# Four loads of q by GpSimd around DMA engine 4, where two had been

## The chip, the cores and the metric

The kernel runs on one core of one Trainium2 chip. The metric is the device time of one execution in microseconds (us), lower is better. The profiled span is about 1.8 us shorter than the time of the same run.

## The reference

Rotary embedding of q and k, then for each batch and head all products of queries with keys. There is no softmax.

```python
batch, seq, heads, dim = 16, 512, 16, 64            # all float32
q_rot = concatenate([q1*cos - q2*sin, q1*sin + q2*cos])   # q1, q2: halves of dim; k likewise
scores = einsum('bshd,bthd->bsht', q_rot, k_rot)    # 16 x 512 x 16 x 512
```

Input is 67 MB, output 268 MB. So this is first of all a kernel that writes.

## The kernel before

A step makes the scores of 128 queries of one batch (four steps to a batch, 64 in all), collects them in one of three stages of 4 MB, and stores that with one DMA issued by SyncE. A stage is used again only when its store has landed whole. A batch of q or k is loaded as one DMA of 128 rows of 16 KB, one row per partition, one batch ahead.

```python
    for i in range(C, NST):                     # the steps from batch 1 on
        ...
        if i % C == C - 2:
            load("q", i // C + 2)
        elif i % C == C - 1:
            load("k", i // C + 3)
    # in scores(i, p), after the last heads of a step:
            dma(SP, nc.sync, o_v[b, i % C], st, f"out{s}", reads=[("st", s, x) for x in range(HP)])
```

One of the 16 DMA engines is slow, and the kernel already takes some work off it: in two batches GpSimd loads 120 rows on fifteen engines, and SyncE the last 8.

```python
    RELIEVED = {("q", 6): 0, ("q", 12): 1}
    SLOW = 4

    def load(which, b):
        ...
        if (which, b) not in RELIEVED:
            dma(SP, nc.sync, ..., dram[which][b], sem, writes=rows + rest)
            return
        n, E, F = 120, C * H * D, C * H * D // 2
        x = RELIEVED[which, b]
        plan.add(POOL, None, (), rows)           # waits, then resets GpSimd's cursor over the engines
        # a dummy of SLOW + 1 = 5 rows: the cursor then stands on engine 5
        ...
        dma(POOL, nc.gpsimd, dst, src, "cursor", writes=[("scratch", x)])
        # 120 rows in halves of 8 KB, on the 15 engines from there: all but engine 4
        ...
        dma(POOL, nc.gpsimd, dst, src, f"part{x}", writes=rows)
        # the last 8 rows, on engines 0 to 7
        dma(SP, nc.sync, t[n:]..., d[n:], sem, writes=rest)
```

## Time and profile before

| what | value |
|---|---|
| time, median of 3 runs | 802.25 us (802.22 to 802.61) |
| profiled span | 799.2 us, of one run of 801.0 us (1.2 us under the median) |
| DMA busy | nine tenths or more in every slice but the first and the last |
| PE, ACT, DVE busy | 86%, 70%, 68% of the span |
| ACT waiting for a store to free a stage | 102.6 us |

The views that carry the argument are in the prediction and are read there. Two things of how to read them. The share of one DMA engine is seen twice in a trace: each DMA leaves sixteen landing records, one for each engine's part, and every packet has a start and a length. Packets don't say which engine moved them. But each starts 3 or 4 ns before the end of the one before it on the same engine, and so they can be strung into sixteen **lanes**. An undisturbed packet of 32 KB (a row of a store) takes 1213 ns, of 16 KB (a row of a load) 611, of 8 KB 309.

### The profile page before, as it was taken

The page shows a single profiled execution, that of the slowest core. Times are in us where ns is not written, and L with a number is a line of the kernel's source. Part 1 is how long each engine was busy: PE and PEld are TensorE (multiplying, and loading weights), DVE is VectorE, ACT ScalarE, POOL GpSimd, SP SyncE. Part 2 cuts the span into 40 slices and gives each one's busy share as a digit, 9 for nine tenths or more (in the row PEclk, how much of TensorE's full clock was granted, in tenths as well). Part 3 has the DMA queues.
Part 4 walks back from the last instruction along what each step waited for, and adds up shares of the span by engine and source line. Part 5 has one row for each costly group of instructions (what it writes and reads, how often), then busy time and mean ns, then how long its engine had stood idle before and what let it go on. Part 6 is the DMA issues. An engine that isn't in the chain of part 4 may idle for free.

```text
span 799.2 us, 8189 instructions
## 1 busy us (share of the span) xinstructions
PE 686.3 (86%) x3072; PEld 297.0 (37%) x3072; DVE 545.2 (68%) x516; ACT 562.5 (70%) x647; POOL 3.5 (0%) x10
## 2 busy tenths in 40 slices
PE   3989998897979979798797987979979799899960
PEld 2444443343434434343343433424434343334320
DVE  6999988586856858577585775857858477585300
ACT  3978886785857858587585875757857687678760
POOL 0000000000000000000000000000000000000000
PEclk9999999898998989899898998988989899899995
DMA  8999999999999999999999999999999999999994
GB/s 346 421 422 424 428 432 427 427 436 430 431 428 431 411 431 426 439 430 433 432 426 433 431 427 431 431 425 420 430 426 436 433 429 434 431 434 403 441 423 180
DMA packets 18033, 335.87 MB, mean 420 GB/s; under 512 B 1904, under 2 KB 3184, under 8 KB 4208
## 3 DMA queue, kind: packets, MB, share of 16 engines
q1 hardware_dynamic: 17120, 331.62, 97.3%
q0 software_dynamic: 608, 3.93, 1.2%
q10 hardware_dynamic: 288, 0.13, 0.1%
q8 instruction: 6, 0.10, 0.0%
q14 instruction: 11, 0.09, 0.0%
HBM read 67.24 MB, written 268.44 MB: 420 GB/s over the span
## 4 chain that ended last, share of the span: by engine, by line
DMA 47%; PE 36%; DVE 8%; ACT 6%; issue 1%; ACTq 0%; DVEq 0%; SPq 0%
DMA out_dram<-st 47%; PE ps L393 27%; PE bank L344 9%; ACT st L402 6%; DVE st L319 3%; DVE part L319 2%; DVE k_sb L319 2%; DVE q_sb L319 1%; DMA sin_t<-in_sin_dram 0%; DVE kT L362 0%; DVE qT L362 0%; ACTq L237 0%; ACT ss_t L439 0%; ACT ss_t L438 0%; ACTq L110 0%
## 5 line engine op out<-in xcount | busy, mean ns | idle before, releaser
L402 ACT COPY st<-ps 128x1024 f32<-128x1024 f32 x512 | 495.7, 1018 | 198.6 <-DMA out_dram<-st 102.6
L393 PE MATMUL ps<-kT,qT 64*128 64x512 f32 x2048 | 544.0, 648 | 71.6 <-ACT st L402 71.6
L393 PEld LDWEIGHTS ps<-kT,qT 64*128 64x128 f32 x2048 | 183.0, 196 | 261.3 <-issue 133.9
L362 DVE COPY qT<-bank 128x512 f32<-128x512 f32 x118 | 81.6, 691 | 199.4 <-PE bank L344 199.4
L344 PEld LDWEIGHTS bank<-ident,q_sb 128*128 128x128 f32 x480 | 55.3, 151 | 102.0 <-issue 98.5
L344 PE MATMUL bank<-ident,q_sb 128*128 128x128 f32 x480 | 86.5, 307 | 1.0 <-DVE q_sb L319 1.0
L344 PEld LDWEIGHTS bank<-ident,k_sb 128*128 128x128 f32 x480 | 50.5, 141 | 94.1 <-DVE k_sb L319 47.5
L344 PE MATMUL bank<-ident,k_sb 128*128 128x128 f32 x480 | 78.7, 287 | 1.6 <-DVE k_sb L319 0.8
L362 ACT COPY kT<-bank 128x512 f32<-128x512 f32 x122 | 72.4, 597 | 6.7 <-PE bank L344 6.7
L319 DVE TENSOR_TENSOR part<-q_sb,ss_t 128x1024 f32<-128x1024 f32 x60 | 73.5, 1225 | 3.1
L319 DVE TENSOR_TENSOR q_sb<-q_sb,cos_t 128x1024 f32<-128x1024 f32 x60 | 73.5, 1225 | 2.1
L319 DVE TENSOR_TENSOR k_sb<-k_sb,cos_t 128x1024 f32<-128x1024 f32 x60 | 73.5, 1225 | 2.0
L319 DVE TENSOR_TENSOR k_sb<-k_sb,part 128x1024 f32<-128x1024 f32 x60 | 73.5, 1225 | 2.1
L319 DVE TENSOR_TENSOR part<-k_sb,ss_t 128x1024 f32<-128x1024 f32 x60 | 73.0, 1216 | 0.3
L319 DVE TENSOR_TENSOR q_sb<-q_sb,part 128x1024 f32<-128x1024 f32 x60 | 72.9, 1216 | 0.0
L344 PE MATMUL bank<-ident,st 128*128 128x128 f32 x64 | 10.8, 318 | 13.3 <-DVE st L319 13.3
L344 PEld LDWEIGHTS bank<-ident,st 128*128 128x128 f32 x64 | 8.2, 161 | 18.6 <-DVE st L319 16.8
L319 DVE TENSOR_TENSOR part<-st,ss_t 128x1024 f32<-128x1024 f32 x8 | 9.8, 1222 | 6.4 <-ACT ss_t L439 6.0
L319 DVE TENSOR_TENSOR st<-st,part 128x512 f32<-128x512 f32 x16 | 11.1, 691 | 0.5
L319 DVE TENSOR_TENSOR st<-st,cos_t 128x1024 f32<-128x1024 f32 x8 | 9.8, 1225 | 0.3
L362 ACT COPY qT<-bank 128x512 f32<-128x512 f32 x10 | 5.7, 615 | 3.5 <-PE bank L344 3.5
L362 DVE COPY kT<-bank 128x512 f32<-128x512 f32 x6 | 4.1, 683 | 0.0
(11 smaller groups left out, 5.5 us busy)
## 6 DMA issues: line engine op xcount, KB each, us to landing
out_dram<-st SPq DMA_DIRECT2D x60, 4096.0 KB, 25.0
k_sb<-in_k_dram SPq DMA_DIRECT2D x15, 2048.0 KB, 27.2
q_sb<-in_q_dram SPq DMA_DIRECT2D x13, 2048.0 KB, 29.7
out_dram<-st SPq DMA_DIRECT2D x16, 1024.0 KB, 13.2
q_sb<-in_q_dram POOLq DMA_DIRECT2D x2, 1920.0 KB, 29.7
st<-in_k_dram SPq DMA_DIRECT2D x1, 1536.0 KB, 8.9
st<-in_q_dram SPq DMA_DIRECT2D x1, 1536.0 KB, 12.1
st<-in_k_dram SPq DMA_DIRECT2D x1, 512.0 KB, 4.6
```

What stands on the lines that cost most here:

```text
L319: plan.add(DVE, one(lambda: nc.vector.tensor_tensor(o, a, b, op=op)), reads, writes, also=more)
L344: done = [nc.tensor.transpose(bank[:, x, :], srcs[x], ident) for x in range(4)]
L362: plan.add(engine, one(lambda: copy(out=dst, in_=src)), [("bank", m)], keys)
L393: nc.tensor.matmul(out=ps[:, r, :], lhsT=lhs[lo:hi, :], rhs=rhs[lo:hi, :], start=True, stop=True)
L402: plan.add(ACT, one(lambda: nc.scalar.copy(out=so, in_=si)), [("ps", y)], [("st", s, p)])
```

## The change

The intent: engine 4 ends last by 7 us. Take more rows from it, by relieving four loads rather than two, spaced evenly; and let the 8 rows that remain go to engines 8 to 15 in every second of them, so that engine 4 doesn't get one and engines 0 to 7 don't get all.

```diff
-    RELIEVED = {("q", 6): 0, ("q", 12): 1}
+    RELIEVED = {("q", 5): 0, ("q", 8): 1, ("q", 11): 2, ("q", 14): 3}
+    tiny = [0]
     SLOW = 4
 ...
+        def move_cursor(k):                      # the dummy, now of k rows
 ...
+        def halves(lo, hi, keys, sem):           # rows lo to hi by GpSimd, in halves of 8 KB
 ...
         plan.add(POOL, None, (), rows)
 ...
-        dma(POOL, nc.gpsimd, dst, src, f"part{x}", writes=rows)
-        dma(SP, nc.sync, t[n:].rearrange("p c (h d) -> p c h d", h=H), d[n:], sem, writes=rest)
+        if x % 2:
+            move_cursor(8)
+            halves(n, P, rest, f"rest{x}")       # the rest on engines 8 to 15
+        move_cursor(SLOW + 1)
+        halves(0, n, rows, f"part{x}")
+        if not x % 2:
+            dma(SP, nc.sync, t[n:].rearrange("p c (h d) -> p c h d", h=H), d[n:], sem, writes=rest)
```

More of the change, by code (lines that the diff above doesn't have):

```diff
@@ L277, in load @@
         x = RELIEVED[which, b]
-        plan.add(POOL, None, (), rows)
-        src = bass.AP(q.tensor, 512 * x, [(512, SLOW + 1), (64, 2), (1, 2)])
-        dst = scratch[: SLOW + 1, 4 * x : 4 * x + 4].rearrange("p (a b) -> p a b", a=2)
-        dma(POOL, nc.gpsimd, dst, src, "cursor", writes=[("scratch", x)])
-        d = dram[which][b]
-        src = bass.AP(d.tensor, d.offset + F, [(E, n), (-F, 2), (1, F)])
-        dst = bass.AP(t.tensor, t.offset + F, [(t.ap[0][0], n), (-F, 2), (1, F)])
-        dma(POOL, nc.gpsimd, dst, src, f"part{x}", writes=rows)
-        dma(SP, nc.sync, t[n:].rearrange("p c (h d) -> p c h d", h=H), d[n:], sem, writes=rest)
+        d = dram[which][b]
+        def move_cursor(k):
+            y = tiny[0]
+            tiny[0] += 1
+            src = bass.AP(q.tensor, 512 * y, [(512, k), (64, 2), (1, 2)])
+            dst = scratch[:k, 4 * y : 4 * y + 4].rearrange("p (a b) -> p a b", a=2)
+            dma(POOL, nc.gpsimd, dst, src, "cursor", writes=[("scratch", y)])
+        def halves(lo, hi, keys, sem):
+            src = bass.AP(d.tensor, d.offset + lo * E + F, [(E, hi - lo), (-F, 2), (1, F)])
+            v = t[lo:hi]
+            dst = bass.AP(v.tensor, v.offset + F, [(v.ap[0][0], hi - lo), (-F, 2), (1, F)])
+            dma(POOL, nc.gpsimd, dst, src, sem, writes=keys)
+        plan.add(POOL, None, (), rows)
+        if x % 2:
[5 more added lines that the diff above has]
+            dma(SP, nc.sync, t[n:].rearrange("p c (h d) -> p c h d", h=H), d[n:], sem, writes=rest)
     def src_keys(which, n):
```

## The prediction

> **What bounds the kernel now.** I read the page first (what moved the data and how evenly), then the chain of waits in the last 110 us, then the totals of waits, then the single landings and packets in the trace.
>
> The page, sections 2, 3 and 4 (mean busy share of the 16 DMA engines in 40 slices, GB/s of the same slices, queues, traffic, and the chain by engine):
>
> ```profile
> DMA  8999999999999999999999999999999999999994
> GB/s 346 421 422 424 428 432 427 427 436 430 431 428 431 411 431 426 439 430 433 432 426 433 431 427 431 431 425 420 430 426 436 433 429 434 431 434 403 441 423 180
> ...
> q1 hardware_dynamic: 17120, 331.62, 97.3%
> q0 software_dynamic: 608, 3.93, 1.2%
> ...
> HBM read 67.24 MB, written 268.44 MB: 420 GB/s over the span
> ...
> DMA 47%; PE 36%; DVE 8%; ACT 6%; issue 1%; ACTq 0%; DVEq 0%; SPq 0%
> ```
>
> The DMA engines are busy in every slice but the last; PE (86%) and ACT (70%) are not full. 335.87 MB at about 430 GB/s is 781 us of the 799.2 us span. The traffic does not change here, so only its distribution over engines can be worth anything. The last slice (180 GB/s) is where that shows: some engines have finished, others have not.
>
> The chain of waits from 690 us (start, length, what):
>
> ```profile
> 695.19 22.85 DMA out_dram<-st
> ...
> 737.24 1.13 PE ps L393 x4
> ...
> 746.35 21.44 DMA out_dram<-st
> ...
> 767.87 5.93 ACT st L402 x7
> ...
> 774.20 1.09 ACT st L402
> ```
>
> A 4 MB store takes 22.85 and 21.44 us to land. The last store is issued at 775.32 and lands 21.65 us later, at 796.97; 2.2 us of closing work make the span. A store lands when its slowest sixteenth does. The sixteen landing records of each DMA, in us after its issue, sorted:
>
> ```
> issue   what       sixteen shares
> 508.06  store      18.40 18.43 18.52 18.54 18.55 18.56 18.68 18.91 21.01 21.16 21.27 22.22 22.37 23.51 23.55 28.48
> 558.98  store      17.50 17.52 17.64 17.70 17.76 17.89 17.96 18.39 18.95 19.12 19.50 20.69 20.94 21.35 22.05 25.18
> 679.21  store      13.52 13.57 13.62 13.68 13.69 13.81 13.89 14.31 15.19 15.47 16.22 17.26 17.42 17.59 18.11 23.97
> 775.32  last store 11.74 11.76 11.80 11.81 11.81 11.82 11.86 11.87 11.88 11.93 12.59 13.14 13.45 13.99 14.69 21.65
> ```
>
> One share is far behind: 21.65 against 14.69 for the next, **6.96 us that only one engine works in**. The packets explain it. They carry no engine number, but each starts 3 or 4 ns before the end of the one before it on its engine, so they chain into lanes. From 400 to 472 us most lanes move 26.7 to 27.05 GB/s (a 32 KB packet takes 1213 ns), and one moves 26.42, with 43 of its 80 packets slow. None of them pauses. Around the relieved load at 527 us that slow lane alone carries no 8 KB packet of the GpSimd load: it is the engine the kernel already steers around, number 4 in the code.
>
> The relief that exists (the GpSimd timeline, start and length in us; the last bracket is the wait before it):
>
> ```profile
> 228.14 0.69 POOL L237 DMA_DIRECT2D scratch<-in_q_dram  x1 [226.62 <-PE bank L344]
> 228.82 0.75 POOL L237 DMA_DIRECT2D q_sb<-in_q_dram  x1
> 526.51 0.58 POOL L237 DMA_DIRECT2D scratch<-in_q_dram  x1 [296.94 <-PE bank L344]
> 527.09 0.75 POOL L237 DMA_DIRECT2D q_sb<-in_q_dram  x1
> ```
>
> Each pulls the lag in (28.48 minus 23.55 = 4.93 us at 508; 25.18 minus 22.05 = 3.13 us at 559), and it grows back: 5.86 us at 679, 6.96 us at the end.
>
> **What the Trainium skill says.** "DMA: Bandwidth & Descriptors", section "Why a DMA increments its semaphore by 16 and not by 1": a copy uses the largest k up to 16 that divides its slowest dimension; a hardware-queue copy runs on the lowest-numbered k engines, a GpSimd one with k under 16 on k consecutive engines from a round-robin cursor. So 120 rows go to 15 engines from the cursor, and a dummy of 5 rows puts the cursor on 5, so that engine 4 is left out. The trace agrees: 480 packets of 8 KB, two a row, 16 on each of 15 lanes per load, none on the slow one. Section "Where 436 GB/s comes from" puts the ceiling at 435.2 GB/s; a clean lane of 27.05 GB/s times 16 is 433, so nothing is to be won above that. Section "Latency and other measured facts" says that engines 7 and 15 are usually slower; the trace disagrees, as the slow lane is one of the five that the 5-row dummy touches (its packets there are 16 bytes, elsewhere 8). "SBUF — State Buffer", section "SBUF: two separate sides", warns that GpSimd's descriptor writing can be blocked by VectorE; here its loads take 0.75 us to issue and 29.7 us to land, as those of SyncE do (29.7), so no sign of it.
>
> **The change, part by part.** A normal q load is 128 rows of 16 KB, 8 rows per engine.
>
> *Removed from engine 4.* Before: batches 6 and 12, 7 rows off each (the 8-row rest still puts one on it): 14. After: batches 5 and 11 in the same way (7 each), batches 8 and 14 with the rest on engines 8 to 15 (8 each): 30. The difference is 16 rows of 16,384 B = 262,144 B; at the lane's 26.42 GB/s that is **9.9 us**, all on the path, since this lane never pauses. Its end goes from 796.97 to about 787.1.
>
> *Added to the others.* Engines 0 to 3 and 5 to 7 get one row from each of two rests, before and after: nothing new. Engines 8 to 15 get one row from each of two rests, before none: 2 x 626 ns (mean of the 16 KB packets) = 1.25 us.
>
> *Who ends last then.* The next two lanes end at 775.32 + 14.69 = 790.01 and 789.31. Followed through the second relief, two lanes next behind engine 4 were one of engines 5 to 7 (it gets a single row of the rest) and one of 8 to 15 (it does not). Which is which at the end I can't tell; I give 1.25 us to the earlier: 790.0 and 790.6. They have their own backlog, so an earlier issue of the last store doesn't move them.
>
> *Cost of a relieved load.* 8 KB packets average 319 ns, 638 a row against 626: 0.1 us per load. More weight: 16 KB reads slow down in a burst when the lanes are close together and enter a load at one time (272 to 274 us, up to 1934 ns instead of 611; excess 0.75 us per engine; slice 14 shows 411 GB/s), and around 545 to 553 (0.65 us). Both follow a relief. Two more reliefs, partly with such a burst: I choose +0.7 us.
>
> *Issuing.* GpSimd gets 10 more instructions, none over 1 us, on an engine idle 99%; two SyncE issues go. Off the path.
>
> Sum: 790.6 + 0.7 = 791.3 against 796.97, **minus 5.7 us**; 802.25 - 5.7 = 796.5 us.
>
> **The rivals.** (1) *The middle lanes become the bound earlier.* The mean of the last landing over all lanes is 775.32 + 13.0 = 788.3, so even a perfect split gains 8.7 us (1.1%). If bursts follow all four reliefs and hit the late lanes, 1.5 to 2 us more: 798. For it: the bursts seen. Against: they came in other places too (75 us). (2) *Compute takes the tail.* From 719 to 746 us the chain is PE and ACT, stores 10 us apart. If that run starts no earlier, little is won: 800. Against: it begins with the store of 695.19 landing at 718.04, whose other 15 shares were in by 711.86, so it moves up by up to 6 us. (3) *Loads from GpSimd jump the queue.* They interleave with waiting stores, and the store issued at 220.74 took 30.2 us rather than 26 to 28. If a stage comes free too late, all engines pause: 1 us each, 798. Against: no lane paused there before. (4) *No late lanes but engine 4:* if the lag of the others comes from accidents early in the run, they may be reshuffled and the end nears 788.5: 794.
>
> **Range and chances.** 796.5 us, 793.8 to 799.5 in 8 of 10: the low end is rival 4, the high end rivals 1 and 3 together. Over 2% faster needs 786.2, below the perfect split: 0.01. Slower by 2% would need a new stall of 16 us: 0.02. Within 2%: 0.97.
>
> **What would show it.** The last store's largest landing falls from 21.65 to 15 or 16 us, with the gap to the next under 2 us (engine 4 no longer last); last slice above 180 GB/s; 960 8 KB packets from 120-row loads plus 32 from the two small rests, none on the slow lane; ACT's wait for stores (102.6 us in all) shorter. Wrong if the gap stays at 5 us or more (a relief removes less than counted), if idle gaps appear in the lanes, or if dips like the 411 GB/s of slice 14 follow all four loads.

## The result, and the profile after

The changed kernel took **798.6 us** (median of 4 runs, 797.49 to 799.53) against 802.24 (4 runs, 801.46 to 802.61). The ratio is 0.9955, 95% interval 0.9938 to 0.9973: within 2%, so the same by that measure, but a small gain that the interval keeps clear of zero. (Ratios are the mean time of one kernel's fast runs over that of the other's fast runs of the same rounds, so not quite the ratio of the medians quoted.) It is 2.1 us above the predicted 796.5 and inside the range. A second set of 6 runs in later rounds gave 798.98 and 0.9962.

A trace is of one run: that of before of a run of 801.0 us, 1.2 us under the median, that of the changed kernel of one of 798.9, 0.3 us over it. So between the two traces the end moves by 2.1 us only, where the medians differ by 3.6.

The page of the changed kernel, the same parts as shown of before (DMA busy in tenths and GB/s in 40 slices, queues, traffic, chain):

```profile
DMA  8999999999999999999999999999999999999995
GB/s 346 420 424 433 429 418 434 426 434 423 430 413 427 435 434 428 439 421 414 426 427 437 432 435 426 419 428 432 428 431 433 432 429 411 428 432 437 430 433 238
...
q1 hardware_dynamic: 16832, 327.42, 96.5%
q0 software_dynamic: 1376, 8.13, 2.4%
...
HBM read 67.24 MB, written 268.44 MB: 421 GB/s over the span
...
DMA 47%; PE 35%; DVE 8%; ACT 6%; issue 1%; ACTq 0%; DVEq 0%; SPq 0%
```

The last slice moved 238 GB/s where it was 180: the ends of the engines lie closer together. GpSimd's queue moved 8.13 MB where it was 3.93. But there are more dips now: slices 12, 19 and 34 (413, 414, 411) follow the loads of batches 5, 8 and 14, and 419 in slice 26 that of batch 11; before there was one deep dip after a relief, slice 14 (411), and a shallow one after the other, slice 28 (420). Before's slice 37 (403) has become 437; more of that below.

The chain of waits of the changed kernel from 690 us (start, length, what):

```profile
692.42 23.51 DMA out_dram<-st
...
717.07 1.71 PE ps L409 x4
...
745.83 19.87 DMA out_dram<-st
...
765.77 5.93 ACT st L418 x7
...
772.11 1.09 ACT st L418
```

It is the same chain. Its run of PE and ACT begins when the store of 692.42 has landed, at 715.93 (it was 718.04), and the last store is issued at 773.23 (775.32): both 2.1 us earlier.

The timeline of GpSimd in the changed kernel (start and length in us, instruction):

```profile
178.43 0.70 POOL L237 DMA_DIRECT2D scratch<-in_q_dram  x1 [176.91 <-PE bank L360]
179.12 0.75 POOL L237 DMA_DIRECT2D q_sb<-in_q_dram  x1
327.14 0.59 POOL L237 DMA_DIRECT2D scratch<-in_q_dram  x1 [147.26 <-PE bank L360]
327.73 0.57 POOL L237 DMA_DIRECT2D q_sb<-in_q_dram  x1
328.29 0.57 POOL L237 DMA_DIRECT2D scratch<-in_q_dram  x1
328.86 0.76 POOL L237 DMA_DIRECT2D q_sb<-in_q_dram  x1
```

The two forms of relief, as meant: two issues with the rest by SyncE, four with the rest by GpSimd, none over 0.8 us. In the packets of the second form, eight lanes carry 18 of 8 KB, seven carry 16, and one none.

What the change was for is in the landing records of the last store (my ordering of them, us after its issue):

```
kernel   issue    sixteen shares
before   775.32   11.74 11.76 11.80 11.81 11.81 11.82 11.86 11.87 11.88 11.93 12.59 13.14 13.45 13.99 14.69 21.65
changed  773.23   13.71 14.06 14.06 14.08 14.59 14.71 14.85 15.19 15.25 16.32 16.36 16.66 17.45 17.99 18.05 21.63
```

**Engine 4 is still last**, by 3.6 us where it was 7.0. Its end moved from 796.97 to 794.86, by 2.1 us. The prediction had it move by 9.9.

Where the rest went shows in the lanes during a relieved load. While the other fifteen engines move the 120 rows, the lane left out has only stores to do, and they are slow:

```
32 KB packets of the left-out lane in time order, ns (1213 when undisturbed)
before,  load at 228 us:  1376 1501 1558 1473 1473 1498 1500 1518 1528
changed, load at 179 us:  1551 1471 1473 1569 1444 1460 1484 1464 1484 1352
changed, load at 476 us:  1512 ... 1511 1516 1535 1506 1539 1532 ... 1335
```

Over 1213 ns a packet, this **slow spell** costs the left-out lane 2.68 and 2.07 us in the two reliefs of before, 2.71, 2.37, 2.68 and 1.72 us in the four of the changed kernel. A relief takes 7 or 8 rows off it, 4.3 to 5.0 us; 1.6 to 3.2 us of that remain. (The sums take in engine 4's ordinary slowness, packets of 1220 to 1270 ns, for as long as the load lasts. With packets over 1300 ns alone I get 2.5 and 1.4 us before, 2.6, 2.2, 2.2 and 1.3 us after.) It was there in the trace of before all along, in a stretch that I had used only to find the lane without 8 KB packets.

A second account takes all sixteen engines together. Summed over all packets and divided by 16, the time of an engine splits into packets at undisturbed speed (782.0 us before, 782.1 after), what packets took beyond that, and idle time:

```
us per engine                         before   changed
packets beyond undisturbed speed        6.2      7.8
idle from 150 to 780 us                 1.0      0.1
idle from 780 us to the last landing    8.6      5.6
sum                                    15.7     13.5
last landing                          796.97   794.86
```

(Idle time before 150 us, 2.8 us in one and 2.9 in the other, is left out, and so are the 3 or 4 ns by which packets overlap. The tail is counted to the end of the last packet, 0.47 us before its landing.) The sums differ by 2.2 us and the landings by 2.1, so nothing of size is missing. The tail got 3.0 us shorter, 0.9 us of idle went (all of it in before's slice 37, after the store of 695.19 whose last share the chain waited for), and 1.6 us came back as slower packets.

### The profile page after: what moved, and what is told of

Same layout as the page of the kernel before. It is cut to its first block, busy times and chain, and to the rows that moved or that the text cites. A ratio compares the mean times of both kernels' runs of the same rounds, so it can differ in the third digit from the quotient of the medians.

```text
span 797.1 us, 8197 instructions
## 1 busy us (share of the span) xinstructions
PE 684.3 (86%) x3072; PEld 295.4 (37%) x3072; DVE 545.2 (68%) x516; ACT 562.4 (71%) x647; POOL 8.4 (1%) x18
## 3 DMA queue, kind: packets, MB, share of 16 engines
q0 software_dynamic: 1376, 8.13, 2.4%
## 4 chain that ended last, share of the span: by engine, by line
DMA 47%; PE 35%; DVE 8%; ACT 6%; issue 1%; ACTq 0%; DVEq 0%; SPq 0%
DMA out_dram<-st 47%; PE ps L409 27%; PE bank L360 9%; ACT st L418 6%; DVE st L335 3%; DVE part L335 2%; DVE k_sb L335 2%; DVE q_sb L335 1%; DMA st<-in_k_dram 1%; DVE kT L378 0%; DVE qT L378 0%; ACTq L110 0%; DVEq L110 0%; SPq L542 0%; SPq L513 0%
## 5 line engine op out<-in xcount | busy, mean ns | idle before, releaser
L237 POOL DMA_DIRECT2D scratch<-in_q_dram x6 | 3.6, 600 | 615.4 <-PE bank L360 615.4
## 6 DMA issues: line engine op xcount, KB each, us to landing
q_sb<-in_q_dram POOLq DMA_DIRECT2D x4, 1920.0 KB, 32.6
st<-in_q_dram SPq DMA_DIRECT2D x1, 1536.0 KB, 12.2
```

Source lines behind the costliest of these rows:

```text
L237: plan.add(engine, one(lambda: e.dma_start(dst, src)), reads, writes, sem=sem, also=also)
```

## The experiments

Three questions: why does a relief give less than its rows, what do the bursts of slow loads come from, and is there a better split? My theory after the result: a lane that is left out stores slowly as long as the others load, and this eats half of what its fewer rows save. The rivals: engine 4 itself is weak there; the bursts that follow GpSimd's loads eat the gain; the place of the reliefs or the split of the rest decides.

All versions of the kernel are correct; the three bare tests (`m1`, `m2`, `m3`) store a constant, back to back, and only run loads beside it. Their outputs are wrong, which doesn't matter for the times. "End" is the last landing of the profiled run, "lead" how much later it is than the second-last lane. The profiled run is not always near the median: that of e_none took 810.07 us, the slowest of its four, and that of e_five 800.34, 1.4 us over its median.

| run | time, median (range) | ratio to before [95%] | end | lead |
|---|---|---|---|---|
| before (first rounds) | 802.24 (801.46–802.61) | | 796.97 | 6.95 |
| changed | 798.6 (797.49–799.53) | 0.9955 [0.9938, 0.9973] | 794.86 | 3.59 |
| e_after (changed, again) | 798.98 (797.85–800.78) | 0.9962 [0.9949, 0.9975] | 795.23 | 4.37 |
| e_pool16 | 805.97 (805.35–806.46) | 1.0043 [1.0026, 1.0060] | 801.84 | 6.37 |
| e_none | 806.05 (803.96–810.07) | 1.0042 [1.0026, 1.0059] | 806.15 | 4.42 |
| e_even | 799.52 (799.16–801.29) | 0.9969 [0.9950, 0.9987] | 795.38 | 3.71 |
| e_late | 797.56 (796.06–802.61) | 0.9949 [0.9906, 0.9991] | 794.45 | 2.05 |
| e_late_again | 797.12 (795.87–801.51) | 0.9945 [0.9924, 0.9965] | 794.27 | 2.69 |
| e_five | 798.98 (796.81–800.38) | 0.9955 [0.9939, 0.9971] | 796.27 | 3.38 |
| e_seven | 802.66 (801.67–806.14) | 1.0013 [0.9994, 1.0031] | 797.10 | 1.33 |
| e_store2 | 829.02 (827.68–830.37) | 1.0332 [1.0315, 1.0349] | | |

### m1_skip_each: is it engine 4?

Sixty-eight stores of 4 MB, and beside them sixteen loads of 120 rows by GpSimd that leave out engine 0, then 1, and so on.

```python
TESTS = [(e, [(0, 120, (e + 1) % 16)]) for e in range(16)]   # engine left out; first row, rows, dummy's rows
```

> Wrong results on purpose: 68 stores of 4 MB run back to back with no compute, and sixteen GpSimd loads of 120 rows leave out engine 0, 1, ... 15 in turn, one every four stores. In the changed kernel the left-out engine 4 stored slowly beside each such load: 5 to 10 packets of 32 KB at about 1490 ns instead of 1213, 1.3 to 2.6 us in all. Theory 1 (the rows still go into the partitions from which the left-out engine's stores read, only by other engines): whichever engine is left out, the lane without 8 KB packets shows such a spell, 2 to 3 us in each of the sixteen tests. Rival (it is engine 4's own weakness beside GpSimd loads): a spell in the test that leaves out engine 4 alone, under 0.5 us in the others. Also: if one lane is about 2% slower in stores alone, engine 4's weakness does not need loads or compute.

Measured: every left-out lane has the spell. Its cost was, for engines 0 to 15 in order,

```
4.46 3.79 3.75 3.94 3.64 4.70 3.73 3.02 3.50 3.43 3.40 3.87 3.13 3.10 3.98 3.74 us
```

with most stores at 1450 to 1550 ns. (How the packets are strung matters: a second program gave 3.5 to 5.0 us, single lanes up to 1.1 us apart from these, and 4.4 for engine 4.) Engine 4 is not worse than all the rest. The rival falls: any engine that is left out pays, and here, where nothing but stores fills its time, it pays 3.0 to 4.7 us of the 5.0 that 8 rows are worth.

The expectation also asked whether a lane is slow in stores alone. None is: from 727 to 748 us of this test, with only stores in flight, the sixteen lanes average 1213 to 1218 ns. In the kernel one lane is slow with only stores in flight, too (e_pool16, 280 to 300 us: 1240 ns, the other fifteen 1213). And it stops with the compute: in the trace of before, engine 4's packets take 1226 to 1268 ns until the last matmul ends at 773.7 us, and 1213 to 1218 from 775 us on. So engine 4 is not weak at storing as such; it is slow beside something else that the kernel does. What that is, no run shows.

### m2_rows: which rows, or how many?

The same with engine 4 left out and other sets of rows.

```python
TESTS = [(4, [(0, 120, 5)]), (4, [(0, 60, 5)]), (4, [(64, 60, 5)]), (4, [(0, 30, 5)]), ...,
         (4, [(8, 120, 5)]), (4, [(16, 15, 5)]), (4, [(16, 8, 8)]), ...]   # first row, rows, dummy's rows
```

> Wrong results on purpose: the same stream of stores, engine 4 left out of every GpSimd load, but the loads write different rows: 120 from 0, 60 from 0, 60 from 64, 30 from 0, 30, 60 and 90, 120 from 4 and from 8, then short ones (15 rows from 16; 8 rows from 16, 48, 0, 64 on engines 8 to 15; 4 rows from 16 and 64). Theory 1 (a port of a fixed group of partitions is shared): the extra time of the left-out lane's stores is there for the loads that cover that group and is zero for the others, so 60 from 0 and 60 from 64 differ by 2 us or more, or both have half where the group is split. Rival (any GpSimd load slows the lane that takes no part): the extra time follows the number of rows, 2.4 us for 120, 1.2 for 60, 0.6 for 30, wherever they lie.

Measured: 120 rows cost 3.90, 3.88 and 4.05 us (from row 0, 4, 8), 60 rows 2.15 and 1.86 (from 0, 64), 30 rows 0.83 to 0.95 wherever they lie, 15 rows 0.60. Which rows it is makes no difference. Eight rows on eight engines, eight left out, hardly slow a store (1230 to 1290 ns). That last point was not what the run was for, and gave the next one.

### m3_packets: packet size, queue, number of engines

```python
# rows, packets of a row, issuing engine; GpSimd starts at engine 5
TESTS = [(120, 2, "POOL"), (120, 1, "POOL"), (120, 4, "POOL"), (120, 8, "POOL"), (104, 2, "POOL"),
         (88, 2, "POOL"), (40, 2, "POOL"), (35, 2, "POOL"), (24, 2, "POOL"),
         (120, 2, "ACT"), (120, 1, "ACT"), (104, 2, "ACT"), (40, 2, "ACT"), (120, 2, "POOL")]
```

> Wrong results on purpose: the stream of stores again; beside it loads that leave engines out, by GpSimd in 120 rows cut into 2, 1, 4 and 8 packets a row, then 104, 88, 40, 35 and 24 rows (13, 11, 10, 7 and 12 engines), then by ScalarE's hardware queue in 120 rows of 2 and of 1 packets, 104 and 40 rows. Theory 2 (held in step: a left-out engine gets one empty packet for each packet of the others and then stores no faster than they do): its 32 KB stores take as long as one store plus one load packet of the others, about 1510 ns with 8 KB packets, 1820 with 16 KB, 1360 with 4 KB, 1285 with 2 KB; without empty packets, on the hardware queue, 1213. Rival (they contend for something with a fixed price): about 1500 ns whatever the packet, and also on the hardware queue; and the more engines are left out, the less each loses.

Measured, with packets of 8 KB, by the number of engines that load (the largest divisor of the rows up to 16, as the lanes confirm; the rule is in the Trainium skill, "DMA: Bandwidth & Descriptors", section "Why a DMA increments its semaphore by 16 and not by 1"):

```
engines that load            15     13     12     11     10      7
rows                        120    104     24     88     40     35
store on left-out lanes, ns 1541   1449   1434   1422   1360   1236   (mean)
```

It is the **number of engines** that load at one time that sets how slow the stores of those left out become (or the number left out, which these tests can't tell from it); the rows set how long it lasts. A repeat of 120 rows gave 1454, so the single figures are good to some 100 ns, the fall from 15 engines to 7 is not in doubt. Size: 16 KB packets 1630 where my idea of lanes held in step wanted 1820, so that idea fails; 4 KB packets 1362. From ScalarE's hardware queue, 120 rows slow the left-out lane too (1439 to 1535 in the spell), so it is nothing of GpSimd's. (The test meant with packets of 2 KB came out as 4 KB.) What the engines share there, no run shows.

### e_pool16: the same loads by GpSimd, without the relief

```diff
-        if x % 2: ...                            # all from here to the rest by SyncE
+        halves(0, P, rows + rest, f"part{x}")    # 128 rows, all 16 engines
```

> The changed kernel with the same four loads by GpSimd on all sixteen engines: nothing is relieved. By the prediction's sum (0.62 us a row off engine 4) it gives back 30 rows, 18.6 us: about 817 us. By what the traces show (a relieved load nets some 1.5 to 2.7 us, because the left-out engine's stores slow down meanwhile) the kernel before is worth about 4 us over none and the changed one 8: about 806 us. No slow stores of 1490 ns on one lane. If the bursts of slow 16 KB reads after each such load (0.5 to 0.85 us per engine) come from reshuffled lanes, they are gone here; if from GpSimd issuing, they stay.

Measured 805.97. So the 30 rows that the changed kernel takes off engine 4 are worth 7.4 us, **0.25 us a row**, not the 0.62 at which the prediction counted them. Before stands between, with 14 rows and 802.24: 0.27 us a row up to there, and 0.23 for the next sixteen (3.6 us); with the intervals of the two ratios, these two prices are not shown to differ. The last slices of its GB/s row tell where a late engine costs:

```profile
GB/s 347 422 426 437 428 402 430 429 432 430 430 406 434 440 427 426 437 437 412 435 430 435 434 427 435 403 431 434 436 422 438 428 386 418 422 437 373 418 438 199
```

In slices 33 and 37 (386 and 373) the sixteen engines idle for 1.14 and 2.76 us on average: most have run dry, and the next stage is not free to be filled until engine 4 has landed its part of the store before.

### e_none: no load by GpSimd at all

```diff
-    RELIEVED = {("q", 5): 0, ("q", 8): 1, ("q", 11): 2, ("q", 14): 3}
+    RELIEVED = {}
```

> The changed kernel without any relieved load: every q load by SyncE on sixteen engines, no GpSimd transfer at all. Beside the same four loads by GpSimd on sixteen engines (806.0 us) it tells what the path through GpSimd costs by itself: if its loads bring the bursts of slow 16 KB reads (about 0.5 us per engine and load), this one is 1 to 3 us shorter than 806, 803 to 805 us, and the four reliefs are worth less over doing nothing than they seem; if the path is free, 806. By the prediction's 0.62 us a row (14 rows more on engine 4 than before) it would be 811.

Measured 806.05, as e_pool16: issuing the loads by GpSimd costs nothing that shows. The four runs spread from 803.96 to 810.07, so a cost or a gain of a microsecond or two would not be seen. The profiled run is the slowest of them, 4 us over the median. In it, packets beyond undisturbed speed came to 12.2 us per engine. So bursts of slow loads come without any load by GpSimd; that they don't fall without one, as the expectation had considered, is seen in this one run only, and how much of them is the run's own bad luck is open. The account for the runs so far (e_none's column is of that slow run):

```
us per engine                         before  changed  e_pool16  e_none
packets beyond undisturbed speed        6.2     7.8       8.5     12.2
idle from 150 to 780 us                 1.0     0.1       4.6      5.3
idle from 780 us to the last landing    8.6     5.6       7.5      7.2
sum                                    15.7    13.5      20.5     24.7
last landing                          796.97  794.86    801.84   806.15
```

From e_pool16 to the changed kernel (7.0 us at the end), 4.5 us are idle time in the middle of the run and only 1.9 us the tail. That is a part of a relief's worth that the prediction had not seen: once one engine is late enough that a stage comes free late, all the others stop with it. Before had nearly used this up (1.0 us left), so that little was left there for its next rows to win.

### e_even: all four rests on engines 0 to 7

```diff
-    RELIEVED = {("q", 5): 0, ("q", 8): 1, ("q", 11): 2, ("q", 14): 3}
+    RELIEVED = {("q", 5): 0, ("q", 8): 2, ("q", 11): 4, ("q", 14): 6}
```

> The changed kernel with all four rests on engines 0 to 7 by SyncE: undoes the turn to engines 8 to 15. Engine 4 carries two rows more, 1.2 us; engines 8 to 15 two rows fewer, which end earlier anyway. By that, 799.8 us, within 0.3% of the changed kernel. If it is the same or faster than 798.6, the turn to engines 8 to 15 with its second dummy earns nothing.

Measured 799.52, ratio 0.9969; the spells cost 2.48, 2.08, 2.13 and 2.17 us. By the medians the rests by turns are worth about 1 us, and with these intervals not even that is sure.

### e_late and e_late_again: the reliefs later

```diff
-    RELIEVED = {("q", 5): 0, ("q", 8): 1, ("q", 11): 2, ("q", 14): 3}
+    RELIEVED = {("q", 7): 0, ("q", 10): 1, ("q", 13): 2, ("q", 15): 3}
```

> The changed kernel with the four relieved loads at batches 7, 10, 13 and 15 instead of 5, 8, 11 and 14. If a relief's worth depends on how far engine 4 is behind when it comes (it can go fast only until it has caught up), later reliefs are worth more and the last comes 57 us nearer the end: gap between the last two landings under 2 us instead of 3.6, 795 to 797 us. If each relief is worth the same, only the 57 us of growth (2.3 us per 100) count: 797.3 us. If nothing depends on the place: 798.6.

> Four reliefs at batches 7, 10, 13 and 15, timed in the same rounds as the changed kernel. If later reliefs leave less time for the lag to grow back, engine 4's lead over the next lane at the end is about 2 us (it was 2.05, against 3.59 in the changed kernel), and the time is about 1 us less than the changed kernel's. If the position doesn't matter, the same within 0.5 us.

> The changed kernel itself, for a comparison in the same rounds: 798 to 799 us, ratio to before 0.995 to 0.996, engine 4 last by 3 to 4 us.

Measured 797.56, and 797.12 with five rounds, beside 798.98 for the changed kernel in those rounds. Engine 4's lead at the end is 2.05 and 2.69 us, where the changed kernel has 3.59 and 4.37. That agrees with a lag that grows by some 2.0 to 2.5 us per 100 us after each relief: a late one leaves it less time. Both medians are the lowest of all, but the runs spread from 795.9 to 802.6 and the intervals (0.9924 to 0.9965, against 0.9949 to 0.9975) overlap. So it may be 1 to 2 us better than the changed kernel, and is not shown to be.

### e_five: one relief more

```diff
-    RELIEVED = {("q", 5): 0, ("q", 8): 1, ("q", 11): 2, ("q", 14): 3}
+    RELIEVED = {("q", 4): 0, ("q", 7): 1, ("q", 10): 2, ("q", 13): 3, ("q", 15): 4}
```

> Five relieved loads (batches 4, 7, 10, 13, 15) in place of four. If a relief nets engine 4 about 2.2 us at the end, and costs each other engine about 0.5 to 0.8 us (its share of the rest, and the burst), engine 4 ends about 2 us earlier than in the changed kernel (794.86 there), near 793, and the next lane at 792 to 793: the two meet, and the time is 796 to 797.5 us. If the reliefs were worth what the prediction counted (0.62 us a row), engine 4 would end 4 to 5 us earlier and no longer be last. If the bursts bind, nothing is gained: 798 or more.

Measured 798.98, as the changed kernel in the same rounds: a miss. Five spells cost 2.25, 2.79, 2.48, 2.51 and 2.59 us, and the end is not earlier (796.27, in a run 1.4 us over the median). At the last four of its reliefs, engine 4's lag behind the mean of the others fell by no more than 0.5 to 1.3 us each. Why these reliefs netted less than the 2.2 us that I had taken for one is open. No gain of a fifth relief shows; by the intervals (0.9939 to 0.9971, against 0.9949 to 0.9975) one of 1 or 2 us can't be excluded.

### e_seven: few engines at a time

If the number of engines that load at one time makes the spell, loads on seven engines should relieve engine 4 at nearly the full price. Eight batches: 35 rows by GpSimd on seven engines (5 to 11, or 12 to 2, or 13 to 3), 80 rows by SyncE on all sixteen, 13 rows by GpSimd around engine 4. It saves engine 4 24 rows.

```diff
-        if x % 2: ...
+        move_cursor((SLOW + 1, 12, SLOW + 1, 13)[x % 4])
+        halves(0, 35, rows, f"part{b % 2}")
+        move_cursor(2 if x % 2 else 9)
+        halves(115, P, last, f"last{b % 2}")
+        dma(SP, nc.sync, t[35:115].rearrange("p c (h d) -> p c h d", h=H), d[35:115], sem, writes=rest)
```

> Eight loads of q (batches 5, 6, 8, 9, 11, 12, 14, 15) of which 35 rows come by GpSimd on seven engines at a time (5 to 11, then 12 to 2 or 13 to 3), 80 rows by SyncE on all sixteen (5 each), 13 rows by GpSimd around engine 4. Engine 4 gets 5 rows of each instead of 8: 24 rows fewer in all (30 in the changed kernel), most others get 4 more. If a left-out engine's stores slow down only when many engines load at one time (35 rows on 7 engines: 1236 ns in the bare test), the slow spell is nearly gone, a row taken off is worth close to 0.6 us, and engine 4 ends at most 2 us behind the mean of the others, no longer last; the other lanes carry 2.5 us more, so 796 to 798 us. If the slowing follows the rows that others load alone, whatever the number of engines, about 0.7 us of spell each, engine 4 ends 4 to 5 us behind the mean: 797 to 800. If each relief costs the same 2 to 2.7 us, nothing is left of it and the time is 801 or more.

The page of this kernel, the DMA issues (line's operation, KB each, median us to landing) and GB/s:

```profile
GB/s 345 419 422 440 426 409 425 428 434 436 415 431 407 411 431 431 433 427 426 431 404 434 426 438 427 422 430 404 430 434 427 439 419 437 425 415 410 435 427 292
...
q_sb<-in_q_dram SPq DMA_DIRECT2D x8, 1280.0 KB, 30.1
q_sb<-in_q_dram POOLq DMA_DIRECT2D x8, 560.0 KB, 21.5
q_sb<-in_q_dram POOLq DMA_DIRECT2D x8, 208.0 KB, 26.1
```

The theory held for the lane: **the spell is gone.** 1037 stores that stand next to no GpSimd packet, on the lanes left out, averaged 1221 ns during these loads, and the last slice rose to 292 GB/s. Engine 4 is no longer last: the lane that is carries packets of the last 35-row load, as far as the lanes can be followed. But the time was 802.66, not 796 to 798. The account says why: packets beyond undisturbed speed 11.3 us per engine (7.8 in the changed kernel), idle 1.0 (0.1), tail 3.0 (5.6). Dips of the GB/s row that follow reliefs (407 and 411, 404, 404 in slices 13, 14, 21 and 28) are bursts of slow 16 KB loads again; the 409 of slice 6 comes before the first relief, and the 410 of slice 37 goes with 0.9 us of idle time. GpSimd makes sixteen loads here, six in the changed kernel, and slow packets cost 3.5 us per engine more; I had left them out of this expectation. Whether the many small loads cause the bursts, no run shows.

### e_store2: relieve a store instead

Stores have rows of 32 KB, so leaving engine 4 out of two of them saves as much with fewer interventions.

```diff
-    RELIEVED = {("q", 5): 0, ("q", 8): 1, ("q", 11): 2, ("q", 14): 3}
+    RELIEVED = {}
+    STORED = {29: 0, 57: 1}      # of these stores, 120 rows by GpSimd around engine 4, 8 rows by SyncE
 ...                              # the code that issues them is left out here
```

> The same relief with stores in place of loads: of stores 29 and 57, GpSimd writes 120 rows around engine 4 and SyncE the last 8 rows, so that engine 4 carries 14 rows of 32 KB less (17 us at 1.24 us each); no q load is relieved. If the left-out engine slows down because the others read from HBM meanwhile, there is no slow spell here and most of the 17 us counts: gap of the last two landings under 2 us, 794 to 797 us, faster than both kernels. If being left out costs whatever the others do, the spell is there (stores of over 1400 ns on the slow lane alone) and the time is 799 to 802.

Measured 829.02, over 3% slower, where I had hoped for 794 to 797. Its page:

```profile
GB/s 344 424 424 433 433 414 433 433 429 429 433 433 424 432 430 431 428 429 327 297 360 433 429 436 435 427 433 402 427 428 424 408 399 430 430 315 291 355 431 261
...
q0 software_dynamic: 352, 7.86, 3.6%
```

Around each of the two stores the whole core falls to some 300 GB/s for three slices, with packets of 32 KB of up to 6.8 us on many lanes; 29.7 us per engine beyond undisturbed speed in all. Two stores in flight at once from two queues are something else than a load beside a store. Why was not looked into.

## Why the prediction was right or wrong

**The total: right, within its range, 2.1 us off, and in part by luck.** Two errors of different size stood behind a sum that was cut off by the next lane, which hid most of the larger: engine 4 ended 7.8 us later than counted (794.86, not 787.1), but only 3.6 us later than the sum's 791.3. And 1.5 of these 3.6 us vanish in the times, because the prediction set a trace of a run of 801.0 us against a median of 802.25, and the changed kernel's trace is of a run 0.3 us over its median: from trace to trace the gain was 2.1 us where 5.7 were predicted.

- **What bounds the kernel: right.** The DMA engines stay full, and the page's other engines did as before.
- **"16 rows ... 9.9 us, all on the path, since this lane never pauses. Its end goes from 796.97 to about 787.1": the step that failed.** The lane doesn't pause, and yet it loses time: while the others load without it, its stores take 1450 to 1550 ns. Before had 4.75 us of this in its two reliefs, the changed kernel 9.48 us in its four: 4.7 of the 9.9 us are lost there (4.4 with packets over 1300 ns alone). The landing moved by 2.1 us. Of the 3.1 us that are left, slower packets in general are up to 1.6 (the mean over all engines); I can't follow one lane through the whole run, and the rest is open. The time per row in the runs is 0.25 us (e_pool16 to changed), where 0.62 was counted. The prediction's own table held the sign: over before's second relief (the stores of 508 and 559 us) the lag fell by 1.8 us, about 2.9 if some 1 us of growing back is added (an estimate from 2.2 us per 100), and 7 rows had been counted at 4.3. That the time falls when the spell goes is not shown: e_seven removed the spell, engine 4 was no longer last, and the time did not fall, with more slow packets elsewhere.
- **"Who ends last then": wrong in its conclusion, right in its number.** The next lane was to end at 790.6 + 0.7 = 791.3; it ended at 791.27 (790.86 in the second trace). It just isn't the last: engine 4 ends 3.59 us after it.
- **The bursts, +0.7 us chosen: too small.** Packets beyond undisturbed speed grew by 1.64 us per engine, of which the added spells, on one lane of sixteen, are 4.7 / 16 = 0.3. They followed all four reliefs, as rival 1 had it. But e_none shows more of them, in a run 4 us over its median, with no GpSimd load at all, so the link that the prediction drew, from relief to burst, is not shown as a cause. It had named dips after all four loads as a sign of being wrong, and that sign came.
- **Issuing by GpSimd off the path: right, as far as the spread shows.** The medians of e_pool16 and e_none are 806 us both.
- **Rival 1 (middle lanes bind, bursts after all four):** the bursts came, the middle lanes don't bind. **Rival 2 (compute takes the tail):** no; its run of PE and ACT began 2.1 us earlier, with the store ahead of it, as argued. **Rival 3 (engines pause for a stage):** no, idle from 150 to 780 us fell from 1.0 to 0.1 us; GpSimd's big loads did land later (median 32.6 us, 29.7 before). It was before that had such a pause, at 720 to 740 us, which I had missed. **Rival 4 (the others get reshuffled):** no.
- **The signs named.** Hit: last slice above 180 GB/s (238), 992 packets of 8 KB and none on the slow lane, no idle gaps. Missed: the last store's largest landing stays at 21.63 us (15 or 16 predicted), since its issue moved along with engine 4; the gap is 3.59 us (under 2 predicted); ACT's wait for stores did not get shorter:

The group of ACT's copies into a stage, before and then changed (busy, mean ns of one, idle before them and what ended most of it):

```profile
L402 ACT COPY st<-ps 128x1024 f32<-128x1024 f32 x512 | 495.7, 1018 | 198.6 <-DMA out_dram<-st 102.6
```

```profile
L418 ACT COPY st<-ps 128x1024 f32<-128x1024 f32 x512 | 495.5, 1018 | 196.7 <-DMA out_dram<-st 103.3
```

A wait of 103 us is where the DMA bound shows in ACT. As I read it, it is set by the mean rate of the engines, which the change hardly touched, and so says nothing of their split; no run tested that.

## What to carry to other kernels

When one engine of a group is relieved, measure what the relief does to that engine while it lasts: here it gave back half of its rows' worth, and the packets of the kernel before had shown that in the two reliefs which it already had. Before steering around a slow member, ask what makes it slow: here, in the traces, it was slow only while the kernel computed. Count a late member also by what it makes the others wait for (a stage freed late idles all sixteen), and expect that part of the gain to end once that wait is gone (argued here from idle times; the times alone don't show it). And a split by fewer engines at a time cured the slow spell itself, but came with more slow packets elsewhere: check the sum over all engines, not the lane that was to be helped.

## What the Trainium skill lacked or had wrong

- "DMA: Bandwidth & Descriptors", section "Latency and other measured facts", names engines 7 and 15 as usually slower. In this case it is engine 4: 26.42 GB/s against 26.7 to 27.05 on most others.
- No page has an engine that is slow only in part of a run: engine 4's store packets average 1244 ns from 400 to 472 us and take 1213 to 1218 once the compute has ended, and with nothing but stores in flight in `m1` all lanes average 1213 to 1218.
- No page says that an engine left out of a load slows down in its stores meanwhile: 1213 ns becomes 1450 to 1550 for a packet of 32 KB when fifteen engines load, 1236 when seven do, on each of the sixteen engines, from GpSimd's queue and from ScalarE's.
- No page has the bursts of slow loads: 16 KB packets of up to 1.9 us instead of 0.61 on all lanes at one time, 0.5 to 1 us per engine each. With the other slow packets they make 6 to 12 us per engine in a run of 800.
- No page warns of a large store by GpSimd beside stores by SyncE: around each of two of 120 rows of 32 KB, the core fell from 430 to about 300 GB/s, and the kernel lost 27 us.
- "SBUF — State Buffer", section "SBUF: two separate sides": nothing to mend. It warns that VectorE can block GpSimd's descriptor writing while it runs in a two-port mode, as for an fp32 copy from SBUF to SBUF. VectorE is 68% busy here, but with products and sums of two tensors and with copies out of PSUM, so the warning is not tested: GpSimd's issues in the changed kernel stayed at 0.57 to 0.76 us, and the kernel with these loads by GpSimd on all engines (e_pool16) took the time of that with SyncE alone (805.97 and 806.05 us).
